# GLA tiles on the right side of SBUF, early output weights, and norm tiles in PSUM in a two-block kernel

## The chip, the cores and the metric

The kernel runs on one core of one Trainium2 chip. The metric is the device time in microseconds (us) of one execution. The core has five engines with a queue each, and every queue runs in order: TensorE (PE, matmuls), VectorE (DVE), ScalarE (ACT), GpSimd (POOL) and SyncE (SP), which issues all the DMA transfers here. On-chip memory is SBUF, with a left side and a right side on which the program stacks its pools, and PSUM, in banks of 128 x 512 f32, into which PE writes.

## The reference, cut to what matters

The model takes 256 context tokens and 256 latent tokens of 1024 features. A first block has two layers. Each layer modulates both streams, mixes the tokens, adds the result through a gate, and then does the same with a feed-forward net with a convolution in it:

```python
for layer in range(DEPTH):
    mod_l = (jax.nn.silu(c) @ mod_w[layer] + mod_b[layer])[:, None, :]
    mod_c = (jax.nn.silu(c_ctx) @ mod_w[layer] + mod_b[layer])[None, None, :]
    sh1l, sc1l, g1l, sh2l, sc2l, g2l = jnp.split(mod_l, 6, axis=-1)
    ...
    hl = modulate(xl, norm_mix_g[layer], sh1l, sc1l)
    ...
    if layer % 2 == 0:
        yc, yl = even_mixer(hc, hl, ...)     # GLA and mLSTM, then concatenate(...) @ w_out
    else:
        yc, yl = odd_mixer(hc, hl, ...)      # SSD
    xl = xl + g1l * yl
    hl = modulate(xl, norm_ffn_g[layer], sh2l, sc2l)
    xl = xl + g2l * conv_ffn(hl, ...)        # up, convolution, silu gate, down
    ...
```

`modulate` is an RMS norm times `1 + scale` plus `shift`. The context stream runs through the feed-forward net of the first layer only. A second block of hybrid layers follows; the change leaves its code alone.

## The kernel before, in words

**Number formats.** Nearly every large matmul is done in three passes: weights and activations are each split into an f16 part and a bf16 rest (`whi`, `wlo`; `hh`, `hl`), and `proj_fm` adds hi x hi, hi x rest and rest x hi in one PSUM bank (L332). `get_w` makes a weight: a DMA by SP into `st` (f32), a conversion on ACT to `whi`, and a subtraction `wlo = st - whi` on DVE, or on POOL where `eng` is given (L294). The modulation can also use f32 weights as they come (`whole`): 64 matmuls per part of the modulation, with `cs` and `st` as operands and 32 columns each (L505), a copy of the sums on ACT (`mrow`) and four small matmuls (L514).

**Layer 0 mixer** (`layer0_mixer`). On the left side of SBUF lie three pools: `gp` (GLA tiles), `ev` (with `yf`, `mqk` and `vext`) and `mp`. The GLA runs first, then `mlstm_inputs`, then `mlstm` with four heads one after another. A head makes scores, `nd` matmuls, denominators `den` and products `hm`; it multiplies by `yf` (`hm<-yf,hm`, L303), normalises (`hsq`, `hss`, `r`, `hm<-hm,r`), transposes (`yT`) and splits into `hh` and `hl`. Modulation (0,2), (0,3) and (0,4) run as f32 fill beside the heads. Then the output: `w` has four parts of `even_o`. The first two belong to the GLA half, whose eight wide groups (`eo`, 12 matmuls of 512 columns each) run beside the heads; the last two belong to the mLSTM half, whose groups (24 matmuls of 256 columns, 4 for each stream) need the last head. Each group ends with residuals `xT<-eo,modc,xT` on DVE, two of 256 columns for a wide group. `xT` is a pool of its own, opened when the mixer's left pools are closed, so it takes a place that one of them held, and its load waits for the last use of that place. After the groups of stream 0 comes the norm of stream 0 (`norm_stream`, in `rstd_bc` and `norm_h`: squares, `ssq`, `r`, `dg`, `rbc`, scaled x `nt`, then `hh` and `hl`), and at the end modulation (0,5), the gate of the net's output.

**First net** (`ffn(0)`). Per iteration i of 22 the up loop takes one weight tile `w_up`, makes two 512-column results, convolves them on DVE and ACT, gates them on POOL and splits the product; beside it runs modulation of layer 1 in half tiles from the pools `ms` and `mp` (`next(mods)`). The first three iterations are begun by stream 0 alone. **SSD** (`layer1_mixer`): its four groups g take five weight tiles each (x, B and C, two of z). **Second net** (`ffn(1)`): the latents alone, with the norm at its head (`norm_h` called from `ffn`).

**Order.** The program text gives dependencies; a scheduler of the framework lays out each engine's queue from them. A tile's place is reused when the last reader of the tile before has finished, and a DMA into it waits for that in SP's queue, with all later DMAs behind it.

Of the kernel before, what the change touches and what calls it, by code (L numbers as in the profile page):

```python
# [248 lines left out]
class Program:  # L249
# [104 lines left out]
    def rstd_bc(self, src, t0, n, tag="nb"):  # L354

        nb = n // 128
        sq = self.nrm.tile([128, 512], F32, tag="sq", name="sq", bufs=1)
        for k in range(8):
            if k == 0:
                self.act(sq[:, :n], src[:, 0, t0:t0 + n], AF.Square)  # L360
            else:
                s2 = self.nrm.tile([128, 512], F32, tag="s2", name="s2")
                self.act(s2[:, :n], src[:, k, t0:t0 + n], AF.Square)
                self.tt(sq[:, :n], sq[:, :n], s2[:, :n], ALU.add)
        ps = self.ps(tag, "ssq")
        for b in range(nb):
            self.T.matmul(ps[:, b:b + 1], sq[:, b * 128:b * 128 + 128], self.ones[:, 0:1], start=True, stop=True)
        v = self.cols.tile([128, nb], F32, tag=f"v{nb}", name="v")
        r = self.cols.tile([128, nb], F32, tag=f"r{nb}", name="r")
        self.ts(v, ps[:, :nb], 1.0 / 1024, EPS, ALU.mult, ALU.add)  # L370
        self.rsqrt(r, v, nb)
        dg = self.nrm.tile([128, 4, 128], F32, tag="s2", name="dg")
        self.tt(dg[:, :nb], bc(self.ident, 1, nb), bc(r, 2, 128), ALU.mult)
        pb = self.ps(tag, "rbc")
        self.T.matmul(pb[:, :n], self.ones, dg[:, :nb].rearrange("p b t -> p (b t)"), start=True, stop=True)
        return pb

    def norm_h(self, src, t0, n, segs, h, pb=None, ks=range(8), o=0, tag="nb"):

        if pb is None:  # L380
            pb = self.rstd_bc(src, t0, n, tag)
        for k in ks:
            t = self.nrm.tile([128, 512], F32, tag="nt", name="nt")
# [103 lines left out]
    def mod_steps(self, l, r, tag="mm", eng=None, pool=None, parts=None, whole=False, halves=False):  # L487
# [5 lines left out]
        for b in range(4):  # L493
            src = self.I["mod_w"][6 * l + r - 2, b]
            if whole:
# [3 lines left out]
            for k in range(2):  # L499
                if halves:  # L500
                    both = self.get_w(src[:, 1024 * k:1024 * k + 1024], 1, 1024, eng(), pool, parts, 1024)
                    terms = [(self.c3, w) for w in both]
                for i, (c, w) in enumerate(terms):
# [23 lines left out]
    def norm_stream(self, l, which, s, tag="nb"):  # L527

        self.norm_h(self.xT, 256 * s, 256, self.segs(l, which, ((s, 0, 256),)), self.h, o=256 * s, tag=tag)
# [8 lines left out]
    def layer0_mixer(self):  # L538
        h, I = self.h, self.I
        with ExitStack() as ph:  # L540
            gp = self.pool("gp", 1, None, ph)
# [9 lines left out]
            self.gla(gp, h, I["even_w"], yf)  # L551
            self.mlstm_inputs(h, I["even_w"], mqk, vext, yf)
            for i in range(4):
                self.split(h[0][:, i], h[1][:, i], yf[:, i])
            self.mlstm(mp, h, mqk, vext, yf)
# [4 lines left out]
        with ExitStack() as tail:  # L560
            tw = self.pool("tw", 2, None, tail)
            w = [self.get_w(I["even_o"][b], 4, 512) for b in range(2)]
# [3 lines left out]
            w += [self.get_w(I["even_o"][b], 4, 512, parts=tw) for b in (2, 3)]  # L566
# [7 lines left out]
            for s in range(2):  # L574
# [8 lines left out]
                if s == 0:  # L583
                    self.norm_stream(0, 1, 0, "ml")
            for _ in self.mod_steps(0, 5, pool=tw, whole=True):
                pass
# [386 lines left out]
    def ffn(self, l, streams):  # L973
# [15 lines left out]
        else:  # L989
            self.norm_h(self.xT, t0, n, self.segs(l, 1, streams), h)  # L990
# [16 lines left out]
        with ExitStack() as ph:  # L1007
# [6 lines left out]
            if both:  # L1014
# [3 lines left out]
                                                          halves=True) for r in range(6))  # L1018
            for i in range(22):
# [19 lines left out]
                if both:  # L1039
                    next(mods)  # L1040

# [45 lines left out]
    def ssd(self, sp, s2, h, y):  # L1087
# [115 lines left out]
        def inputs(g, d):  # L1203
# [45 lines left out]
            for b in range(2):  # L1249
                w = self.get_w(sw[5 * g + 3 + b], 8, 256)  # L1250
# [751 lines left out]
```

## Time and profile before

| | |
|---|---|
| median of 3 runs | 1648.42 us (1648.13 to 1655.8) |
| profiled execution | 1646.42 us; its span 1644.6 us |
| mean granted clock of TensorE | 0.981 of full speed |
| busy: PE / DVE / ACT / POOL | 1563.6 / 1212.3 / 847.9 / 444.8 us |
| chain that ended last, by engine | PE 81%, DVE 8%, ACT 4%, DMA 3%, issue 3% |
| HBM read | 233.68 MB, 143 GB/s over the span |

The profile is of one execution. The chain is the work that ended last, followed back from the last instruction; where it stands on PE, the engine was working, and where it stands on DVE, ACT or a DMA, PE waited for that. PE is busy nearly everywhere, so its granted clock and the stretches in which it stops are what to look at. Waits of the other engines cost nothing by themselves. The layer 0 mixer ends at about 354 us, the first up loop runs dense from 372 us to some 607 us, the SSD begins about 740 us, and the second net begins about 1053 us.

### The profile page before, as it was taken

Reading aid. Unit: us, or ns where it says so; the run is one execution under the profiler, and the core shown is the slowest. Engines: PE = TensorE matmul, PEld = TensorE weight load, DVE = VectorE, ACT = ScalarE, POOL = GpSimd, SP = SyncE. Lnnn points to the kernel's source line nnn. Section 1 sums busy time; section 2 is a strip of 40 time slices with the busy share of each in tenths; the row PEclk is TensorE's granted clock in tenths of the full one; section 3 lists DMA queues with packets and bytes.
Section 4 is the critical chain, followed back from the end, with each engine's and each line's share of the span. In section 5 each row is a group of like instructions: output and inputs, shape, how many; then the busy total and the mean of one; then the engine's idle time right before and its main releaser. Section 6 shows DMA issues by size and latency. Waiting matters only on the chain.

```text
span 1644.6 us, 31809 instructions
## 1 busy us (share of the span) xinstructions
PE 1563.6 (95%) x12978; PEld 1083.6 (66%) x12978; DVE 1212.3 (74%) x2637; ACT 847.9 (52%) x1390; POOL 444.8 (27%) x264
## 2 busy tenths in 40 slices
PE   6999999889999999998999999699998999999998
PEld 3565875467444444475566667488887887778877
DVE  6888856777877796557878898799977885366734
ACT  4746434334555445435555665356564644566542
POOL 0000000224878740000000000259934312431250
PEclk9999999989999999999999999799999999999999
DMA  9222135752444437532222343335454343433651
GB/s 392 89 103 79 54 126 208 258 183 80 157 149 146 138 122 254 177 120 77 103 78 95 112 141 125 124 121 199 137 194 166 141 167 111 146 116 125 228 168 52
DMA packets 41187, 236.77 MB, mean 144 GB/s; under 512 B 4689, under 2 KB 5457, under 8 KB 21201
## 3 DMA queue, kind: packets, MB, share of 16 engines
q1 hardware_dynamic: 41040, 234.74, 40.6%
q8 instruction: 102, 1.67, 0.4%
q14 instruction: 45, 0.36, 0.1%
HBM read 233.68 MB, written 1.05 MB: 143 GB/s over the span
## 4 chain that ended last, share of the span: by engine, by line
PE 81%; DVE 8%; ACT 4%; DMA 3%; issue 3%; POOL 1%; ACTq 0%; SPq 0%; DVEq 0%; POOLq 0%
PE up L332 19%; PE dn L332 9%; PE sx L332 5%; PE fm L332 4%; PE mg L332 4%; PE br L332 3%; PE mqk L332 2%; PE tm L339 2%; ACT whi L306 2%; PE so L332 2%; DVE wlo L294 2%; PE mod L505 2%; PE sz L332 2%; DVE u L303 2%; PE sc L1664 2%
## 5 line engine op out<-in xcount | busy, mean ns | idle before, releaser
L332 PEld LDWEIGHTS <-whi 128*128 128x128 f16 (+2 forms) x5240 | 511.5, 99 | 253.3 <-issue 38.1
L294 POOL TENSOR_TENSOR wlo<-st,whi 128x2048 bf16<-128x2048 f32 (+2 forms) x101 | 311.7, 3097 | 935.5 <-ACT whi L306 934.8
L306 ACT ACTIVATE whi<-st 128x2048 f16<-128x2048 f32 (+3 forms) x242 | 369.1, 1536 | 253.3 <-PE dn L332 46.6
L332 PEld LDWEIGHTS <-wlo 128*128 128x128 bf16 (+2 forms) x2620 | 258.9, 99 | 127.4 <-issue 13.6
L294 DVE TENSOR_TENSOR wlo<-st,whi 128x2048 bf16<-128x2048 f32 (+4 forms) x141 | 279.0, 1988 | 83.8 <-ACT whi L306 82.1
L303 DVE SCALAR_TENSOR_TENSOR u<-up,fcw,u 128x189 f32<-128x189 f32 (+3 forms) x792 | 297.3, 431 | 49.4 <-ACT u L306 41.5
L332 PE MATMUL up<-hh,whi 128*128 128x256 f16 (+1 forms) x752 | 238.2, 319 | 4.4 <-ACT hh L306 4.1
L332 PE MATMUL up<-hl,whi 128*128 128x256 bf16 (+1 forms) x752 | 238.1, 317 | 2.0 <-DVE hl L303 1.9
L332 PE MATMUL up<-hh,wlo 128*128 128x256 f16 (+1 forms) x752 | 237.7, 317 | 0.0
L332 PE MATMUL dn<-hidh,wlo 128*128 128x256 f16 (+1 forms) x396 | 122.2, 310 | 2.3 <-DVE wlo L294 2.3
L332 PE MATMUL dn<-hidh,whi 128*128 128x256 f16 (+1 forms) x396 | 122.3, 311 | 1.8 <-ACT whi L306 1.8
L332 PE MATMUL dn<-hidl,whi 128*128 128x256 bf16 (+1 forms) x396 | 122.5, 310 | 0.0
L306 ACT ACTIVATE u<-up,ppt,fcw 128x512 f32<-128x512 f32 (+1 forms) x88 | 58.1, 660 | 47.9 <-PE up L332 47.9
L332 PE MATMUL fm<-hh,whi 128*128 128x256 f16 x288 | 78.5, 273 | 0.5 <-DVE xc L303 0.5
L332 PE MATMUL fm<-hh,wlo 128*128 128x256 f16 x288 | 78.6, 273 | 0.0
L332 PE MATMUL fm<-hl,whi 128*128 128x256 bf16 x288 | 78.5, 273 | 0.0
L332 PE MATMUL mg<-hh,wlo 128*128 128x256 f16 x256 | 71.0, 277 | 3.6 <-POOL wlo L294 3.6
L332 PE MATMUL mg<-hl,whi 128*128 128x256 bf16 x256 | 71.0, 278 | 1.2 <-DVE hl L303 1.2
L332 PE MATMUL mg<-hh,whi 128*128 128x256 f16 x256 | 70.7, 277 | 0.9 <-ACT mgt L306 0.9
L339 PEld LDWEIGHTS <-hh 128*128 128x128 f16 x640 | 61.5, 99 | 8.8 <-issue 1.1
L298 POOL TENSOR_SCALAR E<-E,rs 128x128 f32<-128x128 f32 (+1 forms) x48 | 37.1, 786 | 107.3 <-DVE rs L1675 47.9
L294 POOL TENSOR_TENSOR sg<-sg,u 128x512 f32<-128x512 f32 (+1 forms) x44 | 44.2, 1004 | 45.6 <-ACT sg L306 45.3
(539 smaller groups left out, 3050.8 us busy)
## 6 DMA issues: line engine op xcount, KB each, us to landing
st<-in_w_up_dram SPq DMA_DIRECT2D x44, 1024.0 KB, 4.8
st<-in_w_dram SPq DMA_DIRECT2D x25, 1024.0 KB, 4.9
st<-in_mod_w_dram SPq DMA_DIRECT2D x48, 512.0 KB, 4.7
st<-in_w_dn_dram SPq DMA_DIRECT2D x32, 704.0 KB, 4.1
st<-in_ssd_w_dram SPq DMA_DIRECT2D x20, 1024.0 KB, 4.9
st<-in_mod_w_dram SPq DMA_DIRECT2D x16, 1024.0 KB, 6.4
st<-in_w_m_dram SPq DMA_DIRECT2D x32, 512.0 KB, 4.3
st<-in_even_w_dram SPq DMA_DIRECT2D x14, 1024.0 KB, 5.0
```

The costliest lines, as they stand in the source:

```text
L294: (eng or self.V).tensor_tensor(o, a, b, op=op)
L298: (eng or self.V).tensor_scalar(o, a, s1, None, op0=op0)
L303: self.V.scalar_tensor_tensor(o, a, s, b, op0=op0, op1=op1)
L306: self.S.activation(o, i, func, **kw)
L332: self.T.matmul(ps, w[a][:, k, c0:c0 + cw], h[b][:, h0 + k, t0:t1], start=first and k == 0 and i == 0, stop=last and k == nk - 1 and i == 2)
L339: self.T.matmul(ps, h[b][:, k, t0:t0 + 128], w[a][:, k, c0:c0 + cw], start=k == 0 and i == 0, stop=k == nk - 1 and i == 2)
L505: T.matmul(ps[32 * j:32 * j + 32, :256], c[:, 2 * b + k], w[:, 0 if halves else k, 256 * j:256 * j + 256], start=b == k == i == 0, stop=b ...
L1664: T.matmul(ps[:, a:b], q[r, tb * 128:tb * 128 + 128], k[r, 0:b - a], start=True, stop=False)
```

## The change

It has four parts.

1. The pool `gp` goes to the right side and is closed after the GLA. Where it was, `tw` is opened, now with four buffers, and all four parts of `even_o` are loaded, converted on ACT and subtracted on POOL between `mlstm_inputs` and `mlstm`. Before, two parts lay in `wsp` and two were made on DVE after the modulation. So the left side holds `ev` and `mp` alone, and `xT` comes to lie where `yf` lay, the first tile of `ev`.
2. Modulation (0,5) leaves the mixer's end. It becomes `gate` in the first net's up loop, a step in each iteration from i = 14, with f32 half tiles of 512 KB from `ms` (`whole` and `halves`), and a PSUM bank from `mm`.
3. `beside` gives norm tiles a PSUM bank if a tag is given: the squares `s2` and the scaled x `nt` of the norm of stream 0 (tags `gA`, `gF`, free after the GLA) and of the second net's norm (`mm`).
4. The two z tiles of SSD group 0 are subtracted on POOL.

```diff
+    def beside(self, tag, p, name):
+
+        return self.ps(p, name) if p else self.nrm.tile([128, 512], F32, tag=tag, name=name)
...
-                s2 = self.nrm.tile([128, 512], F32, tag="s2", name="s2")
+                s2 = self.beside("s2", p, "s2")
...
-            t = self.nrm.tile([128, 512], F32, tag="nt", name="nt")
+            t = self.beside("nt", p and p[1], "nt")
...
+                if halves and whole:
+                    terms = [(self.cs, self.load_w(src[:, 1024 * k:1024 * k + 1024], 1024, pool, 1024)
+                              .rearrange("p (k n) -> p k n", k=1))]
...
     def layer0_mixer(self):
         h, I = self.h, self.I
+        tail = self.ctx.enter_context(ExitStack())
         with ExitStack() as ph:
-            gp = self.pool("gp", 1, None, ph)
+            gs = ExitStack()
+            gp = self.pool("gp", 1, None, gs, side="right")
...
             self.gla(gp, h, I["even_w"], yf)
+            gs.close()
             self.mlstm_inputs(h, I["even_w"], mqk, vext, yf)
...
+            tw = self.pool("tw", 4, None, tail, side="right")
+            w = [self.get_w(I["even_o"][b], 4, 512, self.G, parts=tw) for b in range(4)]
             self.mlstm(mp, h, mqk, vext, yf)
...
-        with ExitStack() as tail:
-            tw = self.pool("tw", 2, None, tail)
-            w = [self.get_w(I["even_o"][b], 4, 512) for b in range(2)]
+        with tail:
             for r in (2, 3, 4):
                 for _ in self.mod_steps(0, r, whole=True):
                     pass
-            w += [self.get_w(I["even_o"][b], 4, 512, parts=tw) for b in (2, 3)]
...
-                    self.norm_stream(0, 1, 0, "ml")
-            for _ in self.mod_steps(0, 5, pool=tw, whole=True):
-                pass
+                    self.norm_stream(0, 1, 0, "ml", ("gA", "gF"))
...
-            self.norm_h(self.xT, t0, n, self.segs(l, 1, streams), h)
+            self.norm_h(self.xT, t0, n, self.segs(l, 1, streams), h, p=("mm", "mm"))
...
+                gate = self.mod_steps(0, 5, pool=ms, whole=True, halves=True)
...
                     next(mods)
+                    if i >= 14:
+                        next(gate)
...
-                w = self.get_w(sw[5 * g + 3 + b], 8, 256)
+                w = self.get_w(sw[5 * g + 3 + b], 8, 256, None if g else self.G)
```

The queues move at three places of the first seam. A row is an operation, what it writes and reads, the size of what it writes, how many follow one another, and in brackets the engines or DMA queues on whose count it waits.

On SP, before, the load of xT stands among the first modulation tiles, after a wait on PE:

```order
L315 DMA st<-in_mod_w_dram 128x2048 [waits DMAHW3_49,DVE_49,Activation_49]
L315 DMA st<-in_mod_w_dram 128x2048 [waits DMAHW4_49,DVE_49]
L559 DMA xT<-in_xT_dram 128x4096 [waits PE_49]
L315 DMA st<-in_mod_w_dram 128x2048 [waits DMAHW5_49,DVE_49]
L315 DMA st<-in_mod_w_dram 128x2048 [waits DMAHW6_49,PE_49]
```

On SP, now, it stands behind all twelve modulation tiles and six w_up tiles, three of which wait for POOL, and the half tiles behind it wait for PE:

```order
L315 DMA st<-in_w_up_dram 128x2048 [waits DMAHW3_49,PE_49]
L315 DMA st<-in_w_up_dram 128x2048 [waits DMAHW4_49,Pool_49]
L315 DMA st<-in_w_up_dram 128x2048 [waits DMAHW5_49,Pool_49]
L315 DMA st<-in_w_up_dram 128x2048 [waits DMAHW6_49,Pool_49]
L572 DMA xT<-in_xT_dram 128x4096 [waits DVE_49]
L1020 DMA fcw<-in_fcw_dram 128x396 [waits PE_49]
L315 DMA st<-in_mod_w_dram 128x1024 [waits PE_49]
```

The wait of xT on DVE is for the last head's `hm<-yf,hm`; the wait of the first half tile on PE is for the last `eo` group.

On DVE, before, from the last head's multiply by `yf` on, the operations of the norm stand among residuals and two weight subtractions:

```order
L303 SCALAR_TENSOR_TENSOR hm<-yf,hm 128x512
L303 SCALAR_TENSOR_TENSOR xT<-eo,modc_108,xT 128x256 x2
L848 TENSOR_REDUCE hss<-hsq 128x4
L300 TENSOR_SCALAR v<-hss 128x4
L347 TENSOR_SCALAR ri<-v 128x4
L300 TENSOR_SCALAR r<-ri 128x4
L294 TENSOR_TENSOR rt<-r 128x4
L294 TENSOR_TENSOR wlo<-st,whi 128x2048
L303 SCALAR_TENSOR_TENSOR rt<-rt,v 128x4
L303 SCALAR_TENSOR_TENSOR xT<-eo,modc_108,xT 128x256 x2
L294 TENSOR_TENSOR wlo<-st,whi 128x2048
L303 SCALAR_TENSOR_TENSOR r<-rt,r 128x4
```

On DVE, now, the end of the same head (its last rows and what follows):

```order
L294 TENSOR_TENSOR rt<-r 128x4
L303 SCALAR_TENSOR_TENSOR rt<-rt,v 128x4
L303 SCALAR_TENSOR_TENSOR r<-rt,r 128x4
L294 TENSOR_TENSOR hm<-hm,r 128x512
L303 SCALAR_TENSOR_TENSOR hl<-yT,ppt,hh 128x512
L303 SCALAR_TENSOR_TENSOR xT<-eo,modc_108,xT 128x256 x18
```

No subtraction is left there, and no residual comes ahead of the head's end: all of them stand behind it.

On ACT, before, at the norm of stream 0 (`s` are the squares), no weight conversion stands between the `hh`:

```order
L306 ACTIVATE s_4308<-xT 128x256 [waits DVE_49]
L306 ACTIVATE hh<-nt,modc_108 128x256 [waits DVE_49] x2
L306 ACTIVATE s_4311<-xT 128x256 [waits DVE_49]
L306 ACTIVATE s_4314<-xT 128x256 [waits DVE_49,Activation_49]
L306 ACTIVATE hh<-nt,modc_108 128x256 [waits DVE_49] x6
```

On ACT, now, three conversions of half tiles stand between them, the first with a wait on its load:

```order
L306 ACTIVATE hh<-nt,modc_108 128x256 [waits DVE_49] x2
L306 ACTIVATE s_4262<-xT 128x256 [waits DVE_49]
L306 ACTIVATE s_4265<-xT 128x256 [waits DVE_49,Activation_49]
L306 ACTIVATE whi<-st 128x1024 [waits DMAHW4_49,PE_49,Pool_49]
L306 ACTIVATE hh<-nt,modc_108 128x256 [waits DVE_49]
L306 ACTIVATE s_4268<-xT 128x256 [waits DVE_49]
L306 ACTIVATE hh<-nt,modc_108 128x256 [waits DVE_49]
L306 ACTIVATE whi<-st 128x1024 [waits DMAHW5_49]
L306 ACTIVATE whi<-st 128x1024 [waits DMAHW6_49]
L306 ACTIVATE hh<-nt,modc_108 128x256 [waits DVE_49] x12
```

In before the same three stood ahead of the norm, among its squares.

## Rows read from the trace of the kernel before

**Rows 1.** The page, part 1: busy us, share of span, instructions, all engines.

```profile
PE 1563.6 (95%) x12978; PEld 1083.6 (66%) x12978; DVE 1212.3 (74%) x2637; ACT 847.9 (52%) x1390; POOL 444.8 (27%) x264
```

**Rows 2.** The page, part 2: busy tenths of PE in 40 equal slices.

```profile
PE   6999999889999999998999999699998999999998
```

**Rows 3.** Windows, core 0: busy us (instructions) by engine, PEclk, DMA share, GB/s.

```profile
325.00:333.00 8.00, 7.19 (x36) 4.01 (x37) 4.92 (x14) 2.49 (x2) 1.31 (x1) 0.79 0.94 321
354.00:366.70 12.70, 7.74 (x75) 3.96 (x74) 9.52 (x27) 5.37 (x13) 0.00 (x0) 0.73 0.49 182
```

**Rows 4.** Timeline, DVE, 308 to 333 us: start, length, line, operation [idle before].

```profile
308.32 1.32 DVE L294 TENSOR_TENSOR den<-den,guard 128x2 f32<-128x2 f32 x1 [0.89 <-ACT den L306]
...
312.12 0.69 DVE L303 SCALAR_TENSOR_TENSOR hm<-yf,hm 128x512 f32<-128x512 f32 x1
...
315.31 2.29 DVE L294 TENSOR_TENSOR wlo<-st,whi 128x2048 bf16<-128x2048 f32 x1 [0.30 <-ACT whi L306]
...
320.57 4.02 DVE L303 SCALAR_TENSOR_TENSOR r<-rt,r 128x4 f32<-128x4 f32 x1
...
332.22 0.75 DVE L303 SCALAR_TENSOR_TENSOR hl<-yT,ppt,hh 128x512 bf16<-128x512 f32 x1 [1.43 <-ACT hh L306]
```

**Rows 5.** Timeline, PE, 354 to 371 us.

```profile
354.17 1.93 PE L505 MATMUL mod<-st,cs 128*32 128x256 f32 x32
360.25 1.93 PE L505 MATMUL mod<-st,cs 128*32 128x256 f32 x16 [4.15 <-DMA st<-in_mod_w_dram]
...
370.79 0.27 PE L332 MATMUL up<-hh,wlo 128*128 128x256 f16 x1
```

**Rows 6.** Windows, core 0, columns as in rows 3: the up loop.

```profile
400.00:450.00 50.00, 50.00 (x268) 22.36 (x267) 41.74 (x108) 28.80 (x32) 45.62 (x22) 1.00 0.46 169
```

**Rows 7.** Timeline, DVE, 1062 to 1097 us: second net, norm and convolution.

```profile
1062.23 6.39 DVE L303 SCALAR_TENSOR_TENSOR hl<-nt,modc,hh 128x256 bf16<-128x256 f32 x2 [2.05 <-ACT hh L306]
...
1069.59 0.88 DVE L303 SCALAR_TENSOR_TENSOR hl<-nt,modc,hh 128x256 bf16<-128x256 f32 x2 [0.18 <-ACT hh L306]
...
1071.44 0.88 DVE L303 SCALAR_TENSOR_TENSOR hl<-nt,modc,hh 128x256 bf16<-128x256 f32 x2 [0.18 <-ACT hh L306]
...
1075.31 21.43 DVE L303 SCALAR_TENSOR_TENSOR u<-up,fcw,u 128x189 f32<-128x189 f32 x62 [1.13 <-ACT u L306]
```

**Rows 8.** Timeline, ACT, 313 to 337 us: weight conversions.

```profile
313.38 5.49 ACT L306 ACTIVATE whi<-st 128x2048 f16<-128x2048 f32 x3
...
335.99 1.04 ACT L306 ACTIVATE whi<-st 128x1024 f16<-128x1024 f32 x1
```

**Rows 9.** DMA issues, 228 to 372 us: count, KB each, us to landing.

```profile
xT<-in_xT_dram SPq DMA_DIRECT2D x1, 2048.0 KB, 9.6
...
st<-in_mod_w_dram SPq DMA_DIRECT2D x3, 512.0 KB, 4.4
st<-in_w_up_dram SPq DMA_DIRECT2D x1, 1024.0 KB, 4.7
```

**Rows 10.** Tile xT, 200 to 372 us: ns min/median/max, first and last start.

```profile
L303 DVE SCALAR_TENSOR_TENSOR xT<-eo,modc,xT x32: 466/476/485, 300.2 to 355.4; 128x256 f32<-128x256 f32 x32
...
L559 SPq DMA_DIRECT2D xT<-in_xT_dram x1: 425/425/425, 230.3 to 230.3; - x1
```

**Rows 11.** Timeline, POOL, 305 us, then 1060 to 1091: weight subtractions.

```profile
305.55 4.07 POOL L294 TENSOR_TENSOR wlo<-st,whi 128x2048 bf16<-128x2048 f32 x1 [267.38 <-ACT whi L306]
...
1060.08 8.27 POOL L294 TENSOR_TENSOR wlo<-st,whi 128x2048 bf16<-128x2048 f32 x2 [437.08 <-ACT whi L306]
...
1086.62 4.08 POOL L294 TENSOR_TENSOR wlo<-st,whi 128x2048 bf16<-128x2048 f32 x1 [1.07 <-ACT whi L306]
```

**Rows 12.** Timeline, PE, 301 us: two of the wide eo matmuls.

```profile
301.60 0.38 PE L332 MATMUL eo<-hh,wlo 128*128 128x512 f16 x1
301.82 0.38 PE L332 MATMUL eo<-hh,whi 128*128 128x512 f16 x1
```

**Rows 13.** Windows, core 0, columns as in rows 3: the SSD's start.

```profile
764.00:784.00 20.00, 11.96 (x76) 7.65 (x74) 19.70 (x27) 14.84 (x23) 0.00 (x0) 0.89 0.56 190
```

More of the change, by code (lines that the diff above doesn't have):

```diff
@@ L352, in rsqrt, with rstd_bc @@
             self.stt(o, t, 1.5, o, ALU.add, ALU.mult)
-    def rstd_bc(self, src, t0, n, tag="nb"):
+    def beside(self, tag, p, name):
+        return self.ps(p, name) if p else self.nrm.tile([128, 512], F32, tag=tag, name=name)
+    def rstd_bc(self, src, t0, n, tag="nb", p=None):
         nb = n // 128
@@ L376, in rstd_bc, with norm_h @@
         return pb
-    def norm_h(self, src, t0, n, segs, h, pb=None, ks=range(8), o=0, tag="nb"):
+    def norm_h(self, src, t0, n, segs, h, pb=None, ks=range(8), o=0, tag="nb", p=None):
         if pb is None:
-            pb = self.rstd_bc(src, t0, n, tag)
+            pb = self.rstd_bc(src, t0, n, tag, p and p[0])
         for k in ks:
-            t = self.nrm.tile([128, 512], F32, tag="nt", name="nt")
+            t = self.beside("nt", p and p[1], "nt")
             for a, b, A, B in segs:
@@ L494, in mod_steps @@
             src = self.I["mod_w"][6 * l + r - 2, b]
-            if whole:
+            if whole and not halves:
                 terms = [(self.cs, self.load_w(src, 2048, pool).rearrange("p (k n) -> p k n", k=2))]
@@ L499, in mod_steps @@
             for k in range(2):
-                if halves:
+                if halves and not whole:
                     both = self.get_w(src[:, 1024 * k:1024 * k + 1024], 1, 1024, eng(), pool, parts, 1024)
                     terms = [(self.c3, w) for w in both]
+                if halves and whole:
+                    terms = [(self.cs, self.load_w(src[:, 1024 * k:1024 * k + 1024], 1024, pool, 1024)
+                              .rearrange("p (k n) -> p k n", k=1))]
                 for i, (c, w) in enumerate(terms):
@@ L525, in segs, with norm_stream @@
                 for s, a, b in streams]
-    def norm_stream(self, l, which, s, tag="nb"):
-        self.norm_h(self.xT, 256 * s, 256, self.segs(l, which, ((s, 0, 256),)), self.h, o=256 * s, tag=tag)
+    def norm_stream(self, l, which, s, tag="nb", p=None):
+        self.norm_h(self.xT, 256 * s, 256, self.segs(l, which, ((s, 0, 256),)), self.h, o=256 * s, tag=tag, p=p)
     def add_residual(self, ps, l, r, k, streams, base=0):
```

## The prediction

> **What bounds the kernel now.** I read the page first: TensorE (PE) is busy for 1563.6 us, 95% of the span [rows 1], so time can only be won where it waits or runs at the lower clock. The forty slices show where: slices 8 and 9 (288 to 370 us) stand at 8 tenths, and so do slice 19 (740 to 781) and, at 6, slice 26 (1028 to 1069) [rows 2]. In the windows of the first seam PE has a granted clock of 0.79 from 325 to 333, and works 7.74 of 12.7 us at 0.73 from 354 to 366.7 [rows 3]; the reader is to see that the seam is two holes with dense work between. The VectorE (DVE) timeline explains the first: the last head ends at 312.12, but its normalisation ends at 332.22 + 0.75, because two weight subtractions of 2.29 us each and an `r` of 4.02 us (its neighbours take about 0.16) lie in it [rows 4]. The second hole is the modulation (0,5): PE waits 4.15 us for its tiles [rows 5]. Behind the seam the up loop has PE busy 50.00 of 50 us [rows 6]: there, added PE work costs its full length. The last hole that the change touches is the start of the second feed-forward net, where two `hl` take 6.39 us instead of 0.88 [rows 7].
>
> **Part 1, the places and the output weight (GLA tiles to the right, four weight parts early).** It removes two ACT conversions (1.83 each, three in 5.49, [rows 8]) and two DVE subtractions (2.29 each) from the end of the last head; the 20.9 us from 312.12 to 332.97 [rows 4] shrink to the chain itself: square, reduce, twelve small operations, multiply, transpose, split, about 6.5 us by the durations of the same rows without the three long ones. That is the gain intended. But the order of SP shows what the move does to xT. Its 2 MB load was issued at 230.30 and took 9.6 us to land, 60 us before its first use at 300.2 [rows 9, 10]. Now xT's place is the one that `yf` held, so the load waits for the last multiply by `yf` (DVE, 312.12 in the trace of before), and all 32 residuals wait for xT. The eo groups have two PSUM banks, so only 2 of the 8 wide groups can run ahead of it; in before all eight ran beside the last heads.
>
> The sum for this seam, taken to the end of the first 24 up matmuls, which is 371.0 in before (the row at 370.79 is the 24th, [rows 5]). (1) Last multiply: 312.1, less 2.6 for one wide eo group no longer ahead of it, plus 3.8 for two more w_up conversions on ACT inside head 3 (1.83 each by [rows 8], and the gaps), plus 1.2 for one more blocked `den` (1.32 against some 0.16, [rows 4]): 314.5. Bounds: 309.5 (only the 2.6 counts) and 322.3 (two whole POOL subtractions of 4.07 [rows 11], less 0.16 each, on top). (2) It takes 0.69; xT lands 4.7 us (a 1 MB load) to 9.6 us (its own row) later [rows 9]; I take 8, nearer its own row: 323.2. (3) Two residuals of 0.476 free a bank: 324.1. (4) What is left: 6 groups of 12 matmuls at 0.22 (start to start in [rows 12]) and 8 of 24 with half the columns, at 0.109: 15.6 + 20.9 = 36.5 us; 2 us more for the lower clock, since in before 8 us at 0.79 lost 1.7 after a shorter stop [rows 3]; bounds 1 and 3.5: the eo end at 362.6, against 354.2 in before, where modulation (0,5) starts [rows 5]. (5) The first half tiles of modulation (1,0) now lie where the output weight lay: their loads wait for the last eo, land 4.4 us later [rows 9], and the conversion of 1.04 [rows 8] stands on ACT ahead of six of the eight `hh`, two more of 1.04 ahead of four. 4.4 + 1.04 + 1.3 (two `hh`, one square) + 2.08 + 0.9 (two `hh`) + 1.84 (the last `nt`/`hl` pair, at the pace of [rows 7]) + 0.65 (three matmuls at the lower clock) = 12.2: the first 24 up matmuls end at 374.8, **3.8 us later** than in before. With both ends of every step: 5.4 earlier to 14.7 later.
>
> What else this part moves: four subtractions of 4.07 us go to POOL beside the first head, and the first three modulation tiles wait for them; three w_up subtractions move into head 3. Modulation only fills PE's waits there, so I cost that delay at nothing; if a head waits for it, it is in the 322.3.
>
> Here a rule speaks against the change. The trace shows a `den` of 1.32 us that ends when the POOL subtraction that began at 305.55 ends, at 309.6 [rows 4, 11], and two `hl` of 6.39 that end soon after POOL's pair from 1060.08, where a later pair takes 0.88 [rows 7, 11]; the DVE operations with a PSUM input (62 `u` in 21.43 us, [rows 7]) go on without a gap beside POOL's subtraction at 1086.62 [rows 11]. The Trainium skill, page "SBUF — State Buffer", section "Who interferes with whom", states it as one pair of ports held exclusively for a whole instruction: a DVE operation with two SBUF inputs contends with a GpSimd instruction that reads SBUF, one with at most one such input does not. By that rule, and the trace agrees, each of the seven moved subtractions can hold up a head; if it hits twice, the sum ends at the 322.3 and the second rival.
>
> **Part 2, modulation (0,5) in the up loop.** 64 matmuls leave the seam (the 12.7 us window above) and come into a loop where PE is full. At full clock 32 such matmuls take 1.93 us, so 64 some 4.0, plus the four small matmuls behind them, which I put at 0.5: **4.5 us later**; bounds 4.0 and 7.7 (16 in 1.93 us at the lower clock; all in [rows 5]). The eight loads of 512 KB go under a loop whose DMA engines are 46% busy [rows 6], and nothing is converted: no cost. One PSUM bank fewer is left for up from iteration 14; PE was full with seven banks less one, and I count nothing, at most 1.
>
> **Part 3, PSUM for norm tiles.** In the second net `hl` reads `nt` from PSUM and no longer waits for POOL: 6.39 down to 0.88 is 5.5 us, and the 62 `u` that follow leave DVE no gap, so it comes out whole: **5.5 us earlier**, bounds 3 and 6. In the first seam the same change takes the waits out of `sq`; it is in step (5), where conversions, not DVE, come last.
>
> **Part 4, two z-weight subtractions of the SSD to POOL.** DVE is busy 19.70 of 20 us there [rows 13]: it gets back 2 x 2.29 = 4.6, and POOL may block two two-input operations for 4.07 each, 8.1. Between -4.6 and +3.6; taken as 0, about the middle, as nothing in the trace of before stands nearer to one end.
>
> **The sum.** +3.8 + 4.5 - 5.5 + 0 = +2.8. The profiled run took 1646.42 us (span 1644.6 and 1.8 around it), 2.0 below the median of 1648.42; set against the median: 1651.2.
>
> **Rivals.** *First, the chains win (faster).* The heads lose work from DVE (2.29 twice before 243 us) and PE, POOL hits nothing, the last multiply falls at 309.5, xT lands in 4.7 us: seam -5.4, loop +4.5, norm -5.5, SSD -4.6, together -11.0: 1637.4. For it speaks that two long subtractions leave DVE, against it that ACT gets the two conversions of w_up in the last head.
>
> *Second, POOL's lock (slower).* The three w_up subtractions run back to back inside head 3, and two of its two-input operations wait a whole one each: the last multiply at 322.3, the rest as in the sum, so the seam is at +11.6; SSD +3.6; loop +4.5; norm -5.5: +14.2, 1662.6. It decides from a last multiply at about 320 on (316 with the SSD's 3.6). For it speaks the `den` of [rows 4]; against it that in before one such subtraction in head 3 cost only 1.2 us.
>
> *Third, the change doesn't do what it says*: xT in place early after all. The seam would then end about 9 us sooner. The order of SP speaks against that; I count it with the first rival.
>
> **How the numbers follow.** A measurement of this kernel can tell about 0.5% from no change: 8.2 us, 1640.2 to 1656.7. The sum as it stands: 48%, its own range 1642 to 1657. First rival 17%, second 35%. The range goes over all three, without the outer ends of both: 1638 to 1665. So faster 0.17, same 0.48, slower 0.35.
>
> **What would show it.** xT's load issued within a microsecond of the last `hm<-yf` and PE idle until it lands; the last eo near 362; on ACT a wait for the mod tile's load between `hh` two and three; 64 more f32 mod matmuls between 500 and 610 us; both first `hl` of the second net below 0.5 us each; two POOL subtractions near 790 us with longer DVE operations beside them. I would be wrong if xT landed before 312, if the eo end came before 355, or if the up loop did not lengthen.

## The result, and the profile after

The changed kernel takes 1668.86 us (median of four executions, 1667.6 to 1672.2), the kernel before beside it 1650.52 (four, 1648.13 to 1655.8): a ratio of 1.0110 [1.0078, 1.0141] (in brackets, here and below, the 95% interval). It is slower, and 1668.86 lies above the forecast range, which ended at 1665; of the rivals the second (POOL's lock, 1662.6) came nearest. The profiled execution took 1668.12 us with a span of 1666.2, which is 21.6 more than the 1644.6 of before.

The page after, parts 1 and 2 (busy us, then PE's busy tenths and its granted clock in 40 slices), answers to [rows 1, 2].

```profile
PE 1568.8 (94%) x12978; PEld 1086.2 (65%) x12978; DVE 1207.2 (72%) x2631; ACT 848.3 (51%) x1390; POOL 468.4 (28%) x270
...
PE   6999999598999999999899999599998999999998
...
PEclk9999999798999999999999999799999989989999
```

PE is busy 5 us longer for the same 12978 instructions, and slice 8 (292 to 333 us) has fallen to 5 tenths at 0.7 of the clock. The windows of that stretch, after (columns as in [rows 3]):

```profile
300.00:325.00 25.00, 11.28 (x64) 8.08 (x62) 19.57 (x55) 8.43 (x15) 11.69 (x3) 0.82 0.59 208
325.00:350.00 25.00, 19.68 (x81) 8.91 (x82) 8.19 (x20) 0.69 (x1) 0.00 (x0) 0.77 0.16 65
350.00:375.00 25.00, 21.46 (x196) 18.96 (x193) 16.46 (x49) 6.66 (x17) 0.00 (x0) 0.98 0.10 28
375.00:400.00 25.00, 20.84 (x164) 17.70 (x165) 18.12 (x59) 9.72 (x20) 6.48 (x3) 0.81 0.38 142
```

PE idles for more than half of the first window, and from 350 to 375 the DMA engines stand at 0.10: the next weight tiles are asked for at 371.39 only, behind the last eo. What ends the waits is in the timelines of SP and PE, after (with the answer on xT's transfer):

```profile
321.80 0.33 SPq L572 DMA_DIRECT2D xT<-in_xT_dram  x1
```

```profile
xT<-in_xT_dram SPq DMA_DIRECT2D x1, 2048.0 KB, 8.7
```

```profile
308.45 1.63 PE L965 MATMUL nd<-vext,W 128*128 128x129 f32 x6 [7.52 <-DVE modc L294]
...
326.40 1.09 PE L928 MATMUL yT<-ept,hm 128*128 128x128 f32 x4 [5.95 <-DVE hm L294]
331.41 0.58 PE L332 MATMUL eo<-hh,whi 128*128 128x512 f16 x1 [3.92 <-DVE xT L303]
```

xT's load goes out 0.03 us behind the end of the last multiply by `yf` (321.08 + 0.69 below), lands at 330.5, and PE takes up the third eo group at 331.41. In this wait PE had only the last head's transposes (`yT`, 326.40) to do. A longer stop lies ahead of it: at 308.45 PE takes up `nd` after 7.52 us in which DVE stood in two long `den`. Why they are long, and why the last multiply came so late, is told by DVE and POOL, after:

```profile
240.35 3.90 DVE L294 TENSOR_TENSOR yf<-yf,gs 128x512 f32<-128x512 f32 x1
...
249.72 4.70 DVE L294 TENSOR_TENSOR hl<-yf,hh 128x512 bf16<-128x512 f32 x3
...
300.30 3.28 DVE L294 TENSOR_TENSOR den<-den,guard 128x2 f32<-128x2 f32 x1
...
304.21 3.45 DVE L298 TENSOR_SCALAR den<-den 128x2 f32<-128x2 f32 x1
...
321.08 0.69 DVE L303 SCALAR_TENSOR_TENSOR hm<-yf,hm 128x512 f32<-128x512 f32 x1
```

```profile
235.59 17.08 POOL L294 TENSOR_TENSOR wlo<-st,whi 128x2048 bf16<-128x2048 f32 x4 [202.98 <-ACT whi L306]
299.49 8.14 POOL L294 TENSOR_TENSOR wlo<-st,whi 128x2048 bf16<-128x2048 f32 x2 [46.83 <-ACT den L306]
312.23 4.08 POOL L294 TENSOR_TENSOR wlo<-st,whi 128x2048 bf16<-128x2048 f32 x1 [4.60 <-ACT whi L306]
```

The four output weight subtractions on POOL hold DVE's `yf` at 3.90 us (0.67 where POOL is idle). The first two w_up subtractions (4.07 us each, 8.14 together from 299.49) end at 303.56 and 307.63, and the two long `den`, 0.16 and 0.17 us elsewhere, end at 303.58 and 307.66: each was held until a subtraction ended.

The other place is the second feed-forward net. DVE after, which answers to [rows 7]:

```profile
1069.87 3.56 DVE L294 TENSOR_TENSOR sq<-sq,s 128x256 f32<-128x256 f32 x7
...
1078.76 2.84 DVE L303 SCALAR_TENSOR_TENSOR nt<-xT,modA,rbc 128x256 f32<-128x256 f32 x7 [1.38 <-PE rbc L379]
1081.51 2.44 DVE L303 SCALAR_TENSOR_TENSOR hl<-nt,modc,hh 128x256 bf16<-128x256 f32 x6
1083.86 0.48 DVE L303 SCALAR_TENSOR_TENSOR nt<-xT,modA,rbc 128x256 f32<-128x256 f32 x1
```

The two `hl` of 6.39 us are gone, as forecast. But all seven adds of the squares now stand behind the last residual, in one go, where in before only two stood there and five between the residuals; and seven of the eight `nt` come ahead of the first `hl`.

Where the 21.6 us of the two profiled executions lie, by the same landmarks in both: up to the start of the last mqk matmul (152.1 against 153.2 us) -1.1; from there to the end of the 24th up matmul, the **seam**, 232.9 against 217.9, +15.0; from there to the first dn, the up **loop**, 239.9 against 236.2, +3.7; on to the first sx +0.9; the SSD 315.0 against 316.6, -1.6; from the last so to the last up, the **second net**, 132.2 against 133.2, -1.0; to the last dn -2.2; from there to the end +7.9. This last item is the same program in both, at another granted clock. Windows of after, then of before, at the same times (which lie 14 to 22 us earlier in the changed kernel's program):

```profile
1320.00:1360.00 40.00, 38.70 (x303) 33.50 (x303) 37.16 (x53) 17.62 (x23) 7.65 (x6) 0.87 0.39 145
1450.00:1510.00 60.00, 60.00 (x425) 45.17 (x423) 35.06 (x82) 35.53 (x73) 18.83 (x20) 0.89 0.37 135
```

```profile
1320.00:1360.00 40.00, 38.69 (x335) 34.24 (x332) 32.15 (x47) 18.03 (x22) 7.39 (x6) 0.96 0.51 188
1450.00:1510.00 60.00, 60.00 (x458) 46.54 (x458) 35.69 (x85) 39.65 (x76) 14.53 (x18) 0.97 0.34 118
```

PE is as busy in both (38.70 and 38.69 of 40 us, 60 of 60), only at a lower granted clock (0.87 against 0.96, 0.89 against 0.97).

### The profile page after: what moved, and what is told of

It reads as the page before. It is cut to its first block, busy times and chain, and to the rows that moved or that the text cites. A ratio compares the mean times of both kernels' runs of the same rounds, so it can differ in the third digit from the quotient of the medians.

```text
span 1666.2 us, 31813 instructions
## 1 busy us (share of the span) xinstructions
PE 1568.8 (94%) x12978; PEld 1086.2 (65%) x12978; DVE 1207.2 (72%) x2631; ACT 848.3 (51%) x1390; POOL 468.4 (28%) x270
## 4 chain that ended last, share of the span: by engine, by line
PE 79%; DVE 11%; DMA 4%; ACT 3%; issue 2%; POOL 1%; ACTq 0%; SPq 0%; DVEq 0%
PE up L332 19%; PE dn L332 8%; PE sx L332 5%; PE fm L332 4%; PE mg L332 4%; PE eo L332 3%; PE br L332 3%; PE tm L339 2%; DVE u L303 2%; PE so L332 2%; ACT whi L306 2%; DVE wlo L294 2%; PE sz L332 2%; PE mod L512 2%; PE mqk L332 2%
## 5 line engine op out<-in xcount | busy, mean ns | idle before, releaser
L294 POOL TENSOR_TENSOR wlo<-st,whi 128x2048 bf16<-128x2048 f32 (+2 forms) x107 | 337.3, 3164 | 929.9 <-ACT whi L306 597.1
L294 DVE TENSOR_TENSOR wlo<-st,whi 128x2048 bf16<-128x2048 f32 (+5 forms) x135 | 269.9, 2010 | 87.0 <-ACT whi L306 84.9
```

The costliest lines, as they stand in the source:

```text
L294: (eng or self.V).tensor_tensor(o, a, b, op=op)
```

## The experiments

The theory after the result: xT's late place carries most of the loss, POOL's subtractions a smaller part, and the squares in PSUM take back the gain of the second net. The rivals: that POOL's lock alone does it, or part 2. Single executions of one kernel lie up to 16 us apart (1642.33 to 1658.73 in 19 of before), so the readings rest on stretches of the profiled executions (seam and loop repeat within 2 us among kernels that are alike there) and on medians beside before's on the same chip. The seam, the loop and the second net are of one profiled execution each. The seams can be compared because PE does the same work in them: 2283 instructions with part 2, and the 68 of modulation (0,5) more without it (the traces of e1 to e4 lack a few records).

| kernel | median us (executions) | ratio to before | seam | loop | second net |
|---|---|---|---|---|---|
| before | 1650.52 (4) | 1 | 217.9 | 236.2 | 133.2 |
| changed | 1668.86 (4) | 1.0110 [1.0078, 1.0141] | 232.9 | 239.9 | 132.2 |
| e9 | 1666.72 (6) | 1.0102 [1.0064, 1.0139] | 233.5 | 240.3 | 139.4 |
| e1 | 1669.72 (4) | 1.0128 [1.0086, 1.0169] | 232.9 | 240.0 | 139.8 |
| e2 | 1666.23 (5) | 1.0115 [1.0071, 1.0159] | 228.1 | 240.1 | 136.1 |
| e3 | 1660.68 (10) | 1.0077 [1.0047, 1.0107] | 229.0 | 239.8 | 135.8 |
| e4 | 1645.82 (10) | 0.9971 [0.9941, 1.0002] | 210.1 | 240.8 | 139.5 |
| e5 | 1651.26 (10) | 1.0014 [0.9981, 1.0048] | 210.2 | 239.9 | 135.1 |
| e6 | 1660.54 (9) | 1.0082 [1.0052, 1.0112] | 227.9 | 236.6 | 133.1 |
| e7 | 1648.47 (10) | 1.0017 [0.9988, 1.0047] | 219.6 | 236.3 | 135.4 |
| e8 | 1643.21 (10) | 0.9965 [0.9941, 0.9988] | 209.6 | 240.1 | 133.0 |
| e10 | 1648.33 (10) | 0.9982 [0.9954, 1.0010] | 205.7 | 240.3 | 139.5 |
| e11 | 1641.55 (10) | 0.9948 [0.9921, 0.9976] | 210.1 | 240.7 | 129.6 |
| e12 | 1649.31 (10) | 1.0001 [0.9978, 1.0025] | 212.8 | 239.9 | 133.3 |
| e13 | 1636.68 (7) | 0.9926 [0.9901, 0.9952] | 206.7 | 239.9 | 129.8 |
| e14 | 1645.27 (12) | 0.9979 [0.9960, 0.9999] | 219.3 | 236.3 | 129.0 |

**e1: xT onto mqk's place**, whose last reader comes before the last multiply. From the changed kernel:

```diff
-            yf = ev.tile([128, 8, 512], F32, name="yf")
             mqk = ev.tile([128, 8, 512], F32, name="mqk")
+            yf = ev.tile([128, 8, 512], F32, name="yf")
```

> The changed kernel with one swap: mqk is allocated ahead of yf, so that xT comes to lie on mqk, which is read for the last time by the scores of the last head (300.4 us in the changed kernel), not on yf (321.1). Theory (the late load of xT holds up the seam): the load goes out once the sixth w_up load is out, near 316.4 instead of 321.8, eo restarts near 326 instead of 331.4, and all behind it is 5.4 us earlier: about 1663.5. Rival (the seam ends with the head's own chain or with the half tiles on ACT, and xT only fills a wait): within 1.5 us of the changed kernel, about 1668.

A miss for the theory: the load was issued at 320.6, 4.4 us ahead of the last multiply (325.0), and the seam stayed at 232.9, the median at 1669.72. DVE's timeline of e1:

```profile
332.17 0.75 DVE L303 SCALAR_TENSOR_TENSOR hl<-yT,ppt,hh 128x512 bf16<-128x512 f32 x1 [1.99 <-ACT hh L306]
332.84 1.65 DVE L303 SCALAR_TENSOR_TENSOR xT<-eo,modc,xT 128x256 f32<-128x256 f32 x4
```

xT is there 9.4 us after its issue, at 330.0, but the residuals now stand in DVE's order behind the last head's `hl`. A few microseconds sooner bought nothing.

**e2: the first three w_up subtractions on DVE** (in the kernel before, too, they are on POOL), and **e3**: this and e1's edit.

```diff
-                w = self.get_w(I["w_up"][l, i], 8, 256, self.G)
+                w = self.get_w(I["w_up"][l, i], 8, 256)
```

> The changed kernel, but the first three w_up subtractions, which now fall into the last head, are on VectorE instead of GpSimd. Theory (GpSimd's hold on the shared access to SBUF delays the last head): the den waits of 3.28, 3.45 and 1.27 us in the last head go, VectorE works 6.9 us more in its gaps, the last multiply by yf falls near 316 instead of 321, xT with it: about 1664. Rival (the delay is the ACT conversions and the order of the queues): the last multiply stays at 320 to 322 and the time at 1667 to 1670.

> Both edits of the two runs before together. Theory: xT is issued behind the three subtractions on VectorE, near 306 to 309, lands by 318, PE goes on with eo almost without a stop, and the eo end falls near 356 instead of 370: about 1654. Rival (each edit takes away the same wait, so that they don't add): about 1663.

Seams of 228.1 and 229.0: 4.8 and 3.9 less than with the subtractions on POOL. DVE of e2:

```profile
301.15 2.29 DVE L294 TENSOR_TENSOR wlo<-st,whi 128x2048 bf16<-128x2048 f32 x1
...
306.88 0.17 DVE L298 TENSOR_SCALAR den<-den 128x2 f32<-128x2 f32 x1
...
317.16 0.69 DVE L303 SCALAR_TENSOR_TENSOR hm<-yf,hm 128x512 f32<-128x512 f32 x1
```

The subtractions cost DVE three times 2.29 us, and the last multiply still comes 4.5 sooner behind the last mqk (164.5 against 169.0); the stop of 7.52 us ahead of `nd` is 3.11 here. With xT late, the three subtractions on POOL cost about a third of the 15.0 us that the seam lost, not all of it. e3 is a miss (1654 expected, 1660.68 measured): xT's load goes out at 313.1 and lands at 324.0, but the first residual starts at 328.39, again behind the last head's `hl` in DVE's order.

**e4: part 1 undone**, the other parts kept.

```diff
-            gp = self.pool("gp", 1, None, gs, side="right")
+            gp = self.pool("gp", 1, None, ph)
...
-            tw = self.pool("tw", 4, None, tail, side="right")
-            w = [self.get_w(I["even_o"][b], 4, 512, self.G, parts=tw) for b in range(4)]
...
+            tw = self.pool("tw", 2, None, tail)
+            w = [self.get_w(I["even_o"][b], 4, 512) for b in range(2)]
...
```

> The changed kernel with part 1 undone: GLA tiles on the left, xT on their place, output weight parts as before; parts 2, 3 and 4 stay. Theory (part 1 makes the loss, by xT and the last head): the first 24 up matmuls end near 362, 9 us before the 371.0 of the kernel before, since the modulation (0,5) is gone from there; the up loop is 4 us longer, the second net 3 earlier: about 1640. Rival (the loss is spread, or comes from the lower clock elsewhere): above 1655.

The seam is 210.1, 22.8 less than in the changed kernel, and the median 1645.82 against 1647.69 of before beside it, a difference that its interval (0.9941 to 1.0002) doesn't quite set apart from none. Part 1 carries the whole loss of the seam and more. The time expected was about 1640; the second net took 139.5 and not the 3 us less than in before that were reckoned with.

**e5: part 1 with xT early.** Two GLA tiles (X, QK) go to a left pool ahead of `yf`, so that xT's place is free again, and one output weight part lies in the general weight pool.

```diff
+            self.gl = self.pool("gl", 1, None, ph)
...
-            tw = self.pool("tw", 4, None, tail, side="right")
-            w = [self.get_w(I["even_o"][b], 4, 512, self.G, parts=tw) for b in range(4)]
+            tw = self.pool("tw", 3, None, tail, side="right")
+            w = [self.get_w(I["even_o"][b], 4, 512, self.G, parts=tw if b else None) for b in range(4)]
...
-        X = gp.tile([128, 2, 2, 512], F32, name="X")
+        X = self.gl.tile([128, 2, 2, 512], F32, name="X")
...
-        QK = gp.tile([128, 2, 2, 512], F32, name="QK")
+        QK = self.gl.tile([128, 2, 2, 512], F32, name="QK")
```

> The changed kernel with two GLA tiles of 8 KB (X and QK) left on the left side ahead of ev, so that xT comes to lie on them and its load waits for the GLA alone; to make room, one of the four output weight parts lies in wsp. The rest of part 1 stays, POOL's subtractions too. Theory (the late xT keeps PE from the wide eo groups, and that is what the seam loses): the wide groups run beside the last head again, eo ends near 350 instead of 371, the first 24 up matmuls near 361, and with the 4.6 us longer up loop the time is about 1644. Rival (the last head, delayed by GpSimd and ACT, holds up the seam by itself): eo ends after 362, about 1658.

Tile xT in e5 (min/median/max ns, first and last start):

```profile
L303 DVE SCALAR_TENSOR_TENSOR xT<-eo,modc,xT x32: 466/476/484, 307.1 to 359.5; 128x256 f32<-128x256 f32 x32
...
L573 SPq DMA_DIRECT2D xT<-in_xT_dram x1: 542/542/542, 222.2 to 222.2; - x1
```

The load leaves at 222.2, the residuals begin at 307.1, and the seam is 210.2: 22.7 less than changed, and equal to e4. So with xT early part 1 costs the seam nothing, and what is left of it is worth nothing there (+0.1) while POOL does the w_up subtractions. (e5 also moves two GLA tiles and one weight part; the run with xT's place alone is e6.) The subtractions still hold DVE: in e5 the last multiply itself takes 4.02 us and a `den` 2.75, but PE has wide eo groups to do meanwhile and stops for 1.1 to 1.7 us only. The 22.7 us can be taken apart: PE stands still for 30.5 us of the seam in the changed kernel and for 13.5 in e5, 17.0 more, and the other 5.7 are the same matmuls taking longer (202.4 us busy against 196.7). Behind the long stops PE runs at the lower clock: the granted clock is 0.60 from 308 to 314 us and 0.50, the lower of its two levels (1.2 GHz), from 330 to 335, and wide `eo` matmuls start 0.43 us apart there where it is 0.22 in [rows 12].

In absolute time e5 gains less, since it loses elsewhere. Its median, 1651.26, is 5.4 above e4's, and the kernels with this edit reach the last mqk at 159.3 to 165.9 us, the others at 152.1 to 158.1. In these three, and in no other, PE stops for 3.2 to 3.4 us at 63 to 65 us, ahead of `gqk`, and waits for DVE's `X`, one of the two tiles that were moved.

**e6: the late xT alone, put into the kernel before.**

```diff
-            gp = self.pool("gp", 1, None, ph)
             ev = self.pool("ev", 1, None, ph)
+            gp = self.pool("gp", 1, None, ph)
```

> The kernel before with one swap: the pool ev is opened ahead of gp, so that xT comes to lie on yf, as in the changed kernel, and nothing else of the change is made. Theory (xT's place alone makes the loss): the load goes out after the last multiply by yf, only two wide eo groups run ahead of it, the eo end falls near 366 instead of 354, and the time is about 12 us above that of the kernel before: 1660. Rival (it needs GpSimd's subtractions beside the heads): within 4 us of the kernel before.

The seam grows from 218.9 (mean of before, e7, e14) to 227.9, the median by 13 us (1.0082): a late xT suffices to make the kernel slower. Here the 9.0 us are stops alone: PE stands still for 22.6 us against 13.5 in those three, and is busy for 205.3 against 204.6 to 206.0. Inside the change a late xT costs 22.7. There the heads, too, end later (the last multiply 169.0 behind the last mqk, 160.3 in e6, 8.7 more), and with xT behind it the seam moved about as much as the last multiply did (4.8 for 4.5 us in e2, 3.9 for 4.6 in e3 against e1); and a second long stop, the one ahead of `nd`, brings a second stretch at the lower clock, which is in the 5.7 us above. How these shares overlap no run separates.

**e7, e14: the second net alone**, both tiles in PSUM (`p=("mm", "mm")`), or `nt` alone, added to the kernel before (the edit of e14):

```diff
-            self.norm_h(self.xT, t0, n, self.segs(l, 1, streams), h)
+            self.norm_h(self.xT, t0, n, self.segs(l, 1, streams), h, p=(None, "mm"))
```

> The kernel before with the second net's norm alone in PSUM (squares and scaled x in mm banks). First theory, as predicted: the two hl no longer wait for GpSimd, all behind them is 5.5 us earlier: about 1643. Second theory: hl does end 5.5 us earlier, but the squares are added in one go at the end, PE stands still in one piece for longer and runs at the lower clock for longer behind it, over 8 us lost there instead of 5.1, so that the last up matmul is at most 2 us earlier: 1647 to 1651.

> The kernel before with the scaled x of the second net's norm alone in PSUM, its squares in SBUF. Theory: the first u comes 19 us behind the last so matmul instead of 24.3, the last up matmul some 130 instead of 133.2: 3 to 5 us faster than the kernel before, 1643 to 1646. Rival (the gain in e11 was that of a single execution): within 2 us of the kernel before.

The second net takes 135.4 us in e7 and 129.0 in e14, against 133.2: with both, 2.2 lost, with `nt` alone, 4.2 gained. The medians go the same way but say little by themselves: e7's interval holds 1, e14's ends at 0.9999.

**e8, e11: e4 with the second net's norm in SBUF**, or with `nt` alone in PSUM.

> The run e4_no_part1 with the second net's norm in SBUF again: parts 2, 4 and the first norm's PSUM tiles are left of the change. If the second net's norm in PSUM gives its 5.5 us, this is slower than e4_no_part1 (1645.8) by that: 1651. If the lower clock behind it takes it back, the two are within 3 us: 1643 to 1648.

> The run e4_no_part1 with the squares of the second net's norm in SBUF and only the scaled x in PSUM. If the late addition of the squares is what lengthens PE's stop, the clock loses about 5 to 7 us there instead of 12, and the last up matmul comes 128 to 131 us behind the last so matmul (133.2 in the kernel before, 139.5 in e4): about 1641. If it is the earlier start itself that meets the lower clock, 133 to 136: about 1644.

The second net: 139.5 in e4, 133.0 in e8, 129.6 in e11. e8 is not slower than e4 (1643.21 against 1645.82), as it would be if both tiles in PSUM gave 5.5 us. DVE and POOL of e4:

```profile
1059.38 4.07 DVE L303 SCALAR_TENSOR_TENSOR r<-rt,r 128x2 f32<-128x2 f32 x1
1063.48 4.24 DVE L294 TENSOR_TENSOR dg<-ept,r 128x256 f32<-128x256 f32 x1
```

```profile
1059.37 8.07 POOL L294 TENSOR_TENSOR wlo<-st,whi 128x2048 bf16<-128x2048 f32 x2 [285.59 <-DVE rt L303]
```

The squares that come late put the end of the norm's small operations beside POOL's pair of subtractions: `r` and `dg` wait for one each (0.16 and 0.42 elsewhere). In e11:

```profile
1055.92 0.96 DVE L294 TENSOR_TENSOR sq<-sq,s 128x256 f32<-128x256 f32 x2
...
1062.21 2.84 DVE L303 SCALAR_TENSOR_TENSOR nt<-xT,modA,rbc 128x256 f32<-128x256 f32 x7 [1.38 <-PE rbc L379]
1064.96 1.26 DVE L303 SCALAR_TENSOR_TENSOR hl<-nt,modc,hh 128x256 bf16<-128x256 f32 x3
```

```profile
1062.57 8.09 POOL L294 TENSOR_TENSOR wlo<-st,whi 128x2048 bf16<-128x2048 f32 x2 [285.88 <-ACT whi L306]
```

Only two adds stand behind the last residual, and beside POOL's pair lie `nt` and `hl`, which read PSUM and take their usual time.

**e9: the changed kernel again**, unchanged, to see what repeats.

> The changed kernel itself once more, for the 8 us that its profiled execution lost in the second block, where the program is the same (the clock stays low for 11 and 14 us behind a stop where it was 4 us each in the kernel before). If that belongs to single executions, this profile shows some 393 to 396 us from the last down matmul to the end and the times spread down to about 1658. If it belongs to this kernel, the profile shows 403 to 404 us again and no time lies below 1666.

Seam 233.5 and loop 240.3 repeat, and part of the lower clock in the second block does not: from the last dn to the end it is 399.7 us, between the two outcomes expected (393 to 396, 403 to 404), and the times go down to 1659.55, so the 7.9 us there belong in part to single executions. The second net is 139.4 instead of 132.2, with `r` at 4.04 and `dg` at 4.24 us as in e4. So the -1.0 of the changed kernel's profiled execution was luck, and by a hair: there `dg` began 0.03 us ahead of POOL's pair. DVE and POOL of that execution:

```profile
1076.96 0.42 DVE L294 TENSOR_TENSOR dg<-ept,r 128x256 f32<-128x256 f32 x1
```

```profile
1076.99 8.34 POOL L294 TENSOR_TENSOR wlo<-st,whi 128x2048 bf16<-128x2048 f32 x2 [285.81 <-DVE r L303]
```

The nine profiled executions with both tiles in PSUM fall into three groups by how many of these small operations were held: none, 132.2 (the changed kernel); `dg` alone, 135.1 to 136.1 (e2, e3, e5, e7); `r` and `dg`, 139.4 to 139.8 (e1, e4, e9, e10). Their mean is 137.0.

**e12: part 2 alone**, in the kernel before.

```diff
-            for _ in self.mod_steps(0, 5, pool=tw, whole=True):
-                pass
...
+                gate = self.mod_steps(0, 5, pool=ms, whole=True, halves=True)
...
+                    if i >= 14:
+                        next(gate)
```

> The kernel before with part 2 alone: modulation (0,5) in the up loop. Theory: the first 24 up matmuls end near 365 (6 us earlier, as in e4), the loop is 4.5 us longer, the rest as in the kernel before: 1646 to 1647. If the PSUM tiles of the first norm have a share in the 6 us, the first 24 end at 367 to 369 and the time is 1648 to 1650.

The seam is 6.1 shorter than 218.9, the loop 3.7 longer; the median doesn't move (1.0001). The 24th up matmul ends at 367.4, as expected if the first norm's tiles in PSUM have a share in what e4 gains.

**e10: e5 with e2's edit. e13: e10 with `nt` alone in PSUM.**

> The run e5_p1_xt_early with the first three w_up subtractions on VectorE instead of GpSimd. Theory (GpSimd's hold delays the last head, whose last multiply fell at 325 there): the last multiply falls 5 to 8 us earlier, the eo end from 358 to about 352, the first 24 up matmuls to about 365: about 1645. Rival (PE has the eo groups to do anyway, so the head's end does not count): within 2 us of 1651.

> The run e10_xt_early_wup_dve (xT early, w_up subtractions on VectorE) with the second net's squares in SBUF and only its scaled x in PSUM. Theory (the three faults of the change are xT's place, the squares in PSUM and GpSimd's subtractions in the last head): the last up matmul comes about 130 us behind the last so matmul instead of 139.5, the time is 6 to 8 us below e10: 1640 to 1643, below both kernels. Rival (what is won there is lost to the lower clock behind it): 1646 to 1649.

The seams are 205.7 and 206.7, 4.0 under e5 on average, and 3.7 under e4, e8 and e11 (206.2 against 209.9). Whether part 1 has a share in the 3.7 is not shown: e4, e8 and e11 have the w_up subtractions on POOL, and no run has them on DVE without part 1. The way expected for e10 was a miss: the last multiply comes 164.5 us behind the last mqk in e5 and in e10 alike, and it is the eo groups that end sooner (193.7 against 197.4); 1648.33 and e5's 1651.26 lie within the spread of both. e13 takes 1636.68 us, 0.9926 [0.9901, 0.9952], and beats both kernels. Its windows of the seam:

```profile
300.00:325.00 25.00, 23.59 (x159) 14.53 (x158) 21.65 (x61) 12.16 (x26) 0.00 (x0) 1.00 0.63 224
325.00:350.00 25.00, 24.74 (x205) 19.84 (x204) 17.30 (x54) 5.58 (x13) 0.00 (x0) 1.00 0.22 73
```

PE works 48.33 of these 50 us, at the full clock, and 30.96 in the changed kernel. Whether e13 beats e11 (0.9948) by its part 1 can't be told from the medians, whose intervals overlap.

## Why the prediction was wrong

*xT's order (right).* The load followed the last multiply by 0.03 us, and PE stood until it landed but for the last transposes, as the step said. The landing took 8.7 us where 8 were forecast (step 2), freeing a bank 0.92 against 0.95 (step 3), the rest of eo 39.9 against 38.5 (step 4), and the stretch behind it, in which ACT waited for the modulation tile, 13.7 against 12.2 (step 5). These four are 3.6 us too small together. The seam's end was forecast 3.8 us later than in before, and it came 13.9 later.

*Step (1), the last multiply (wrong).* 314.5 forecast, 321.08 measured, 6.6 of the 10.2 us by which the seam's end (385.0 against 374.8) was missed. Two things failed. The four output weight subtractions beside the first head were costed at nothing, with only the modulation in mind; they held two `yf` and the `hl` by 8.2 us altogether on DVE, PE waited 1.9 us, and the first head's multiply came 113.5 us behind the last mqk instead of 108.6. And POOL's w_up subtractions hit two `den` and not one, with 7.52 us of PE idle behind them: this was the second rival. That its 322.3 for the last multiply is close to what came is in part luck, since it has no term for the first head. The forecast chose one hit because one such subtraction had cost 1.2 us in before; but there it began by itself, and here two ran back to back. By the Trainium skill, page "SBUF — State Buffer", section "Who interferes with whom", also `tensor_scalar` can take the shared pair, in a two-port mode, when its operands meet that mode's conditions; the prediction had used only the section's rule on two inputs, and its sentence that one SBUF input does not contend leaves this exception out. The `den` at 304.21, a `tensor_scalar` with one SBUF input that took 3.45 us, agrees.

*The third rival's price (wrong).* It put an early xT at "about 9 us sooner"; inside the change the seam is 22.7 shorter with it (e5), and the 9.0 holds only without the change's later heads (e6). The forecast saw the two banks and the wait, but not that, without the wide eo groups, PE has nothing to do while DVE is held (the 7.52 us), nor the lower clock behind each such stop (5.7 us).

*Part 2 (size right).* +4.5 forecast for the loop; 240.1 against 236.4 on average, +3.8. Its gain in the seam, 6.1 (e12), was never a term of its own.

*Part 3 (wrong).* "So it comes out whole" failed. `nt` in PSUM alone is worth 3.4 to 4.2 (129.8, 129.6 and 129.0 against 133.2), inside the bounds of 3 to 6; but the same edit moves the squares, and that was costed at nothing. The order that comes with it puts the adds behind the last residual and the norm's `r` and `dg` beside POOL's pair, and both tiles together cost 3.8 on average (137.0) where 5.5 were to be gained. In the first seam the change's norm gave 2.9 (209.9 in e4, e8, e11 against 212.8 in e12).

*Part 4 (not contradicted).* Taken as 0; the SSD took 1.6 us less in the changed kernel, 2.3 less in e9. No run has part 4 alone, and the SSD varies by more than that among executions: 313.9 to 320.6 in the eleven with it, 316.6 to 321.7 in the five without, with medians 1.6 apart.

*The sum as measured.* Seam +14.2 (233.1 as the mean of changed, e9 and e1, against 218.9), loop +3.8, second net +3.8, SSD -1.6: +20.2, where the medians say +18.3 and the forecast said +2.8. (The short stretches between them, +0.9 and -2.2 in the two profiled executions, are left out.) The range ended at 1665 because it left out the outer ends, where POOL hits twice and the second net gains nothing; both came. That the second rival's 1662.6 lies near is luck in its terms: it has the seam at +11.6 and the SSD at +3.6, but the second net at -5.5. Its time was given the lower chance (35%) against 48%.

## What to carry over

When tiles change places, look up which load inherits which place: here a 2 MB load that slipped behind the last reader of its new place took all that waits for it along, and took away the work that had hidden the delays ahead of it. An operand that goes to PSUM to get out of POOL's way must be judged with the order that comes with it; here one of two tiles gave 4 us, and the second took back more. In these traces work given to POOL was free where nothing on DVE beside it read two SBUF inputs or was a `tensor_scalar`, or where PE had other work meanwhile (e5).

## What the runs showed of the hardware

A `tensor_scalar` of 128x2, one SBUF input, took 3.45 us instead of 0.17 and ended 0.03 us behind POOL's subtraction; in e12 one of 128x4 (`v`, at 323.41) took 1.97 instead of 0.16 and ended 0.03 us behind another. In the prediction only operations with two inputs waited. Two subtractions that POOL ran back to back (8.14 us) held one `den` each: as the first ended, a waiting DVE operation got through, and the next was held by the second.

The same 1.3 us stop of PE (`hss`, at 1326.99 in before and at 1341.03 in the changed kernel) was followed by different losses of clock in the same program: the stretches of 25 us from 4 us ahead of it have a mean granted clock of 0.93 in before and 0.80 in the changed kernel:

```profile
1323.00:1348.00 25.00, 23.69 (x202) 20.85 (x201) 21.53 (x36) 10.57 (x14) 5.31 (x6) 0.93 0.45 161
```

```profile
1337.00:1362.00 25.00, 23.70 (x173) 20.25 (x172) 21.65 (x36) 9.19 (x13) 5.63 (x6) 0.80 0.41 150
```

From the last dn to the end the executions took 392.7 to 403.7 us, with the longer ones in e11 and e14 as well, which have none of part 1. Why one execution gets the clock back later than another is open.
